# A hybrid conv / SSD diffusion layer on one core: the prompt's norm and eight projections moved ahead of the sample's norm, and the gate products of the scan moved half a chunk later

## The chip, the cores and the metric

The kernel runs on one core of one Trainium2 chip. The metric is the device time of one execution in microseconds. A kernel consists of five instruction queues that run side by side: PE (TensorE, matrix products into PSUM), DVE (VectorE), ACT (ScalarE), POOL (GpSimd, which reads and writes SBUF only) and SP (SyncE, which here only issues DMA transfers). Each queue runs its instructions in the order in which they were written into the program, and an instruction waits on semaphores for the results or free buffers it needs.

## The reference

One layer is applied to two groups of tokens with the same weights: 256 prompt tokens and 1024 sample tokens of width 1024. Cut to what matters here:

```python
mod = silu(c) @ w_ada + b_ada                         # six blocks of 1024: shift, scale, gate, twice
h   = rmsnorm(x, g_norm1) * (1 + scale_m) + shift_m   # over 1024 channels
hc, gb, gc, z, xbc, dtf, dtb = split(h @ w_in)        # 512, 512, 512, 512, 1024, 8, 8 columns
out_a = gb * dwconv1d(gc * hc)                         # short gated convolution
xs, B, C = split(silu(dwconv1d(xbc) + b))              # 512, 256, 256
dt  = softplus(dt + dt_bias); y = ssd(xs, dt, B, C)    # chunks of 128 tokens, forward and backward scan
y   = rmsnorm(y * silu(z), g_ssd_norm)
x   = x + gate_m * (concat(out_a, y) @ w_out)
x   = x + gate_f * convffn(rmsnorm(x) * (1 + scale_f) + shift_f)
```

The prompt uses the modulation of `c_ctx`, the sample that of `c`. The results are the final norms of both groups and the prompt's two final scan states.

## The kernel before, in words

Activations lie transposed: channels on the 128 partitions, tokens along the free dimension. So `x` is eight tiles ("channel blocks", k = 0 to 7) of 128 channels, and a matrix product with `w_in` gives an output tile of 128 channels as a sum over the eight k. Products are made in three passes to keep precision: a weight tile is split into a rounded high part (`whi`, on ScalarE) and the rest (`wlo`, on VectorE or GpSimd), the activation likewise, and TensorE adds high x high, high x low and low x high (`mm3`, L160, L162, L164; all three kinds of operation are recorded at the lines of small helpers such as L77, `tt`, and L80, `stt`). A prompt tile is thus 8 x 3 = 24 products of 256 columns, a sample tile 48 products of 512 columns. `w_in` has 24 output tiles: 12 for the short convolution (`outa`, three for each j), 4 for `z` (`zproj`), 8 for `xbc`; a narrow product gives dt.

The order of the work around the change is the order of the code, arranged by a list scheduler within it (each engine's queue can take a later piece of code first where its inputs are earlier), and by a few hand-set edges (`after`).

1. *Start* (L232 to L264). Both groups' `x` are loaded, ScalarE squares them, TensorE sums the squares over the channels with a matrix of ones (L243, L256), ScalarE makes the reciprocal root by Ln and Exp.
2. *The channel loop* (L310 to L339). For each k, `ada_block(k)` (L277 to L296) loads two pieces of the first two modulation blocks, multiplies them (L284), transposes the result (L290) and makes `mod` and `aff`, the scale of the norm. Then the sample's block k is normalized and split (L320 to L324), and two of the sample's `xbc` tiles (`N_LOOP = 2`) get their products for this k (L332). The prompt's block is normalized as well (L335), and the sample's dt products run at k = 3 and 7.
3. *Prompt tiles*: eight `xbc` tiles (L703), four `z` tiles with the prompt's dt stage (`dtstage`, a chain of small operations between ScalarE and VectorE), and twelve tiles of `outa`.
4. *Sample tiles*: its dt stage, the other six `xbc` tiles (L731), with the other four modulation blocks (`ada`) between them.
5. *The scan.* While chunks of the scan run, `fillers` gives TensorE halves of the sample's `z` and `outa` tiles. `gate(x, c0, n)` makes the norm of `y * silu(z)` of one chunk in three steps: load z; multiply, square and add; sum over channels on TensorE (L800), Ln, Exp and multiply. `post_s(i)` says after which half chunk i each step is written. Then come `w_out` and the feed-forward part.

The tile pools hand out buffers by tag: the PSUM pool has `acc` (two tiles of 1024 columns), `yp` (one) and `sa` (three). A new tile waits until its buffer's last reader is done.

## Time and profile before

| | |
|---|---|
| three runs | 1577.93, 1579.02, 1580.55 us (median 1579.02) |
| profiled execution | 1580.42 us, of which the span from first to last instruction is 1578.5 us |
| granted TensorE clock, mean | 0.991 |
| busy: PE, DVE, ACT, POOL | 1525.0, 1101.3, 662.0, 513.8 us |
| DMA | 191.98 MB, mean 122 GB/s |
| first product of step 3 / L458 of step 4 / first product of `w_out` | 71.2 / 157.5 / 516.1 us |

A row of the timeline has the start in us, the duration in us, the engine, the line, the operation, output and input tiles (numbers left out) with shapes, and how many records were merged; in brackets stands the idle time of the engine before it and what ended it. Two records belong to one product of 32-bit floats with full precision. TensorE's records overlap, so the distance of two starts is the price of one. A row by windows gives, for a stretch of the execution, busy time and number of instructions of PE, PEld (the weight loads), DVE, ACT and POOL, and then the granted clock (1.00 is full speed), the DMA engines' mean busy share and GB/s.

### The profile page before, as it was taken

What the parts mean: (1) busy time and instruction counts of PE and PEld (TensorE: products, weight loads), DVE (VectorE), ACT (ScalarE), POOL (GpSimd) and SP (SyncE); (2) the same over time, 40 slices, a digit from 0 to 9 for tenths busy, and PEclk for the clock granted to TensorE, in tenths of its full rate; (3) what the DMA queues carried; (4) which work ended last, traced back from release to release, by engine and by line L of the source; (5) the groups of instructions that cost most, each with busy time, mean ns of one, the idle gap of its engine ahead of it and who ended that gap; (6) DMA issues with size and microseconds to landing.
All of it is one profiled execution on the core that took longest, in us unless ns stands there. A gap on an engine that the chain in (4) does not pass through costs nothing. (4 is left out here: it accounts for less than half of the span.)

```text
span 1578.5 us, 22525 instructions
## 1 busy us (share of the span) xinstructions
PE 1525.0 (97%) x8722; PEld 1296.2 (82%) x8722; DVE 1101.3 (70%) x1634; ACT 662.0 (42%) x1025; POOL 513.8 (33%) x288
## 2 busy tenths in 40 slices
PE   6988999999999999999999999999999999999997
PEld 2688667777877888888888888888888888888886
DVE  5665615367787339797666598656679978798696
ACT  6553334257777235443332253332334433433333
POOL 1455001111110001343333333333346555445452
PEclk9999999999999999999999999999999999999999
DMA  8555554343434712322222233212252322343221
GB/s 304 214 184 162 216 202 147 111 150 123 144 101 146 286 67 82 112 73 69 66 68 78 66 133 112 70 65 67 76 184 93 102 99 99 106 161 97 93 78 61
DMA packets 86908, 191.98 MB, mean 122 GB/s; under 512 B 9330, under 2 KB 36626, under 8 KB 86802
## 3 DMA queue, kind: packets, MB, share of 16 engines
q1 hardware_dynamic: 80978, 187.41, 34.6%
q10 hardware_dynamic: 5824, 3.15, 0.7%
q8 instruction: 68, 1.11, 0.3%
q14 instruction: 38, 0.31, 0.1%
HBM read 167.37 MB, written 23.15 MB: 121 GB/s over the span
## 5 line engine op out<-in xcount | busy, mean ns | idle before, releaser
L80 DVE SCALAR_TENSOR_TENSOR cc<-acc,sm,cc 128x504 f32<-128x504 f32 (+5 forms) x836 | 545.7, 665 | 110.8 <-ACT cc L983 52.5
L77 POOL TENSOR_TENSOR wlo<-raw,whi 128x1024 fp32r<-128x1024 f32 (+2 forms) x83 | 193.5, 2331 | 672.4 <-ACT whi L151 518.5
L151 ACT ACTIVATE whi<-raw 128x1024 fp32r<-128x1024 f32 x90 | 95.1, 1057 | 243.6 <-PE acc L162 215.6
L80 DVE SCALAR_TENSOR_TENSOR x<-dn,mod,x 128x288 f32<-128x288 f32 (+2 forms) x176 | 96.1, 546 | 95.3 <-PE dn L164 95.1
L77 POOL TENSOR_TENSOR dlo<-draw,dhi 128x512 fp32r<-128x512 f32 (+1 forms) x88 | 108.9, 1238 | 90.8 <-ACT dhi L1036 88.8
L160 PE MATMUL acc<-ya,whi 128*128 128x512 f32 (+1 forms) x400 | 119.2, 355 | 1.4 <-DVE cv L77 1.4
L162 PE MATMUL acc<-ya,whi 128*128 128x512 f32 (+1 forms) x400 | 119.0, 355 | 0.0
L162 PE MATMUL acc<-oa,whi 128*128 128x512 f32 (+1 forms) x400 | 118.9, 355 | 0.0
L164 PE MATMUL acc<-ya,wlo 128*128 128x512 f32 (+1 forms) x400 | 118.7, 354 | 0.0
L164 PE MATMUL acc<-oa,wlo 128*128 128x512 f32 (+1 forms) x400 | 118.6, 354 | 0.0
L160 PE MATMUL acc<-oa,whi 128*128 128x512 f32 (+1 forms) x400 | 118.4, 353 | 0.0
L160 PE MATMUL dn<-yb,dhi 128*128 128x288 f32 (+2 forms) x352 | 110.0, 313 | 5.3 <-DVE x L80 4.1
L77 POOL TENSOR_TENSOR wlx<-raw,whx 128x1024 fp32r<-128x1024 f32 (+2 forms) x32 | 73.7, 2303 | 120.2 <-ACT whx L151 104.5
L162 PE MATMUL dn<-yb,dhi 128*128 128x288 f32 (+2 forms) x352 | 109.6, 311 | 0.8 <-POOL yb L77 0.8
L164 PE MATMUL dn<-yb,dlo 128*128 128x288 f32 (+2 forms) x352 | 109.6, 311 | 0.0
L160 PE MATMUL acc<-h,whi 128*128 128x512 f32 x320 | 105.7, 407 | 0.0
L1036 ACT ACTIVATE dhi<-draw 128x512 fp32r<-128x512 f32 (+1 forms) x88 | 52.9, 602 | 121.5 <-PE dn L162 50.8
L162 PE MATMUL acc<-h,whi 128*128 128x512 f32 x320 | 101.4, 396 | 0.0
L164 PE MATMUL acc<-h,wlo 128*128 128x512 f32 x320 | 100.8, 396 | 0.0
L160 PE MATMUL dn<-g,dhi 128*128 128x288 f32 (+2 forms) x304 | 95.1, 313 | 0.0
L162 PE MATMUL dn<-g,dhi 128*128 128x288 f32 (+2 forms) x304 | 94.8, 312 | 0.3 <-POOL g L77 0.3
L164 PE MATMUL dn<-g,dlo 128*128 128x288 f32 (+2 forms) x304 | 94.8, 312 | 0.0
(340 smaller groups left out, 3628.9 us busy)
## 6 DMA issues: line engine op xcount, KB each, us to landing
raw<-in_w_up SPq DMA_DIRECT2D x88, 512.0 KB, 3.2
x<-in_w_ada SPq DMA_DIRECT2D x32, 512.0 KB, 5.5
draw<-in_w_down SPq DMA_DIRECT2D x64, 256.0 KB, 2.7
x<-in_w_in SPq DMA_DIRECT2D x24, 512.0 KB, 3.3
raw<-in_w_in SPq DMA_DIRECT2D x22, 512.0 KB, 4.2
xs<-in_w_ad SPq DMA_DIRECT2D x16, 512.0 KB, 8.4
csb<-csds SPq DMA_DIRECT2D x16, 512.0 KB, 3.8
raw<-in_w_out SPq DMA_DIRECT2D x16, 512.0 KB, 3.2
```

What stands on the lines that cost most here:

```text
L77: (eng or V).tensor_tensor(out=out, in0=a, in1=b, op=op)
L80: V.scalar_tensor_tensor(out=out, in0=a, scalar=s, in1=b, op0=op0, op1=op1)
L151: act(hi, raw, AF.Copy)
L160: nc.tensor.matmul(o, wh[:, k, :], rh(k), start=k == 0, stop=False)
L162: nc.tensor.matmul(o, wh[:, k, :], rl(k), start=False, stop=False)
L164: mm = nc.tensor.matmul(o, wl[:, k, :], rh(k), start=False, stop=k == n - 1)
L1036: act(wh, raw, AF.Copy)
```

## The change

- *Start.* Only the prompt's `x` is loaded and normalized first. The table that holds Ln and Exp is loaded once, early.
- *Channel loop.* For each k, the modulation block, the prompt's normalized block and the products of **all eight prompt `xbc` tiles** for this k (L301; eight 256-column halves of four PSUM tiles of a new tag `pj`, five buffers). The weight piece of a block is 512 KB in place of 128 KB; its low part is made by VectorE. Behind it, the sample's block of `x` is loaded, squared on ScalarE and added up by **GpSimd**.
- *Sample's norm.* `norm_s`, a generator: sums by TensorE, Ln, Exp, then for each k one `stt` on VectorE (x times scale times factor), one activation (the high part), one `stt` (the low part). Its steps are called between the prompt's `z` and `outa` tiles. The shift is left out of the sample's `x`, so its dt product gets the shift's part by eight one-column products.
- *Prompt tiles.* `xbc` reads the PSUM tiles of the loop. All other prompt tiles use `pj`, and their weights are loaded into four pieces of `xq`.
- *Sample tiles.* All eight `xbc` tiles are here now, and the dt products before them, in a new PSUM pool.
- *The scan.* Step three of `gate` for chunk c - 1 and the prompt's gate steps are written after other half chunks; at the end, the splits of `y` and the last three fillers are written in another order. PSUM pools wait tile by tile where one takes another's place.

```diff
-N_LOOP = 2
...
-        if "space" not in kw:
+        if kw.get("space") != DRAM:
             kw["reuse_waits"] = "tile"
...
+    def pj():
+        return T(ps, [P, 512], "pj", 5)
...
-    xs = [T(nrm, [P, TS], "x", 8) for _ in range(KT)]
-    pr_s = [psa(), psa()]
-    for k in range(KT):
-        dma(xs[k], xT[:, k, TP:TT])
-        q = T(cv, [P, TS], "cv", 4)
-        sq = act(q, xs[k], AF.Square)
...
+    pl = [pj() for _ in range(4)]
+    pxbc = [pl[t // 2][:, TP * (t % 2):TP * (t % 2) + TP] for t in range(8)]
+    xs = []
+    ada_block(0)
+    for k in range(KT):
+        raw = T(wst, [P, KT, P], "raw", 2)
+        dma(raw, A["w_l"][k])
+        wh, wl = wpair()
+        act(wh, raw, AF.Copy)
+        tt(wl, raw, wh.bitcast(F32), ALU.subtract)
+        if k < KT - 1:
+            ada_block(k + 1)
+        q, i = k // 4, k % 4
+        hi, x = hp_hi[q][:, i], xp[q][:, i]
+        act(hi, x, AF.Identity, scale=aff[:, 0, k, 0:1], bias=col(0, k, 0))
+        ts(x, x, aff[:, 0, k, 0:1], col(0, k, 0), ALU.mult, ALU.add)
+        tt(hp_lo[q][:, i], x, hi.bitcast(F32), ALU.subtract)
+        for n, (w, h) in enumerate(((wh, hi), (wh, hp_lo[q][:, i]), (wl, hi))):
+            for t in range(8):
+                mm = nc.tensor.matmul(pxbc[t], w[:, t, :], h, ...)
...
+        x = T(nrm, [P, TS], "x", 8)
+        dma(x, xT[:, k, TP:TT])
+        xs.append(x)
+        sq = T(hsp, [P, TS], "h", 16)
+        act(sq, x, AF.Square)
+        if k == 0:
+            acc_s = sq
+        else:
+            tt(acc_s, acc_s, sq, ALU.add, nc.gpsimd)
...
+    def norm_s():
+
+        rs = T(cv, [P, TS], "cv", 4)
+        for a in range(0, TS, 512):
+            pr = psa()
+            nc.tensor.matmul(pr, ones, acc_s[:, a:a + 512], start=True, stop=True)
+            act(rs[:, a:a + 512], pr, AF.Ln, scale=1.0 / D, bias=epsc)
+            act(rs[:, a:a + 512], rs[:, a:a + 512], AF.Exp, scale=-0.5)
+        for k in range(KT):
+            x = xs[k]
+            stt(x, x, aff[:, 0, k, 1:2], rs, ALU.mult, ALU.mult)
+            hi, lo = [T(hsp, [P, TS], "h", 16, F32R) for _ in range(2)]
+            act(hi, x, AF.Identity, bias=col(0, k, 1))
+            stt(lo, x, col(0, k, 1), hi.bitcast(F32), ALU.add, ALU.subtract)
...
+            yield
...
     for j in range(4):
         zproj(SP, j, PG if j % 2 else PV)
         if j == 0:
             dts = dtstage(SP, d4_p, silu)
+        else:
+            next(norm)
     for j in range(4):
-        for _ in outa(SP, j, PG):
-            pass
-        if j == 0:
+        for i, _ in enumerate(outa(SP, j, PG)):
+            if i % 4 == 1:
+                next(norm, None)
+        if j == 1:
             dttok(SP, *dts)
+    for _ in norm:
+        pass
+    close_pool(g_ps)
...
-    for i in range(N_LOOP, 7):
+    for i in range(7):
         xbc(SS, i, xbcs[i], PV)
...
         if i == 0:
-            next(gate_p)
             next(gates[0])
-        if i == 1:
-            next(gate_p)
         if i % 2 == 1:
             next(gates[c])
-        else:
             if c > 0:
                 next(gates[c - 1])
             if c + 1 < SS.nc:
                 next(gates[c + 1])
+        if i in (0, 3):
+            next(gate_p)
...
-    with tc.high_priority():
-        next(gates[-1])
-    for _ in filler:
-        pass
...
+    split(xall, mya, 0)
+    split(xq[:, :, 0:TA - TP], mya, TP)
+    next(filler)
+    next(filler)
+    next(gates[-1])
+    for _ in filler:
+        pass
+    split(xq[:, :, TA - TP:], myb, 0)
```

The instruction queues show where things stand now. First ScalarE in the channel loop, before. `h` is the sample's normalized high part, `bc` the prompt's, `whi`/`whx` a weight's high part, `cv<-sa` the copy of the modulation products:

```order
L314 ACTIVATE whi_248<-raw_246 128x256
L287 ACTIVATE cv_216<-sa_207 128x256
L321 ACTIVATE h_225<-x_113,mod_80,aff_81 128x1024
L335 ACTIVATE bc_173<-xl_100,mod_80,aff_81 128x256 x2
L314 ACTIVATE whx_293<-raw_291 128x256
L287 ACTIVATE cv_263<-sa_254 128x256
L321 ACTIVATE h_272<-x_114,mod_80,aff_81 128x1024
```

The same place in the change; `h<-x` is now the square of the sample's x:

```order
L271 ACTIVATE cv_220<-sa_211 128x256
L311 ACTIVATE h_257<-x_255 128x1024
L296 ACTIVATE bc_119<-xl_101,mod_78,aff_79 128x256
L290 ACTIVATE whx_262<-raw_260 128x1024
L271 ACTIVATE cv_277<-sa_268 128x256
L311 ACTIVATE h_314<-x_312 128x1024
L296 ACTIVATE bc_119<-xl_101,mod_78,aff_79 128x256
L290 ACTIVATE whi_319<-raw_317 128x1024
```

A block's weight split (L290) stood ahead of its modulation copy and norm (L314 before); it stands behind the norm (L296) now, and a square lies between copy and norm.

Then VectorE behind the prompt's dt stage, at the first `outa` tiles, before (`acc` is PSUM; `cv`, `xl`, `sm` are SBUF):

```order
L77 TENSOR_TENSOR cv_1072<-acc_1080,cv_1072 128x256
L80 SCALAR_TENSOR_TENSOR cv_1106<-cv_1072,sm_63,cv_1106 128x255 x2
L520 TENSOR_SCALAR cv_1155<-cst_66,cep_934 40x40 x2
L77 TENSOR_TENSOR cv_1106<-acc_1116,cv_1106 128x256
L77 TENSOR_TENSOR xl_1144<-cv_1106,xl_1142 128x256
L77 TENSOR_TENSOR cv_1193<-acc_1201,cv_1193 128x256
```

And in the change (`x` the sample's block, `cv_731` the norm's factor, `h` high and low part, `pj` PSUM):

```order
L79 SCALAR_TENSOR_TENSOR x_199<-x_199,aff_79,cv_731 128x1024
L79 SCALAR_TENSOR_TENSOR x_255<-x_255,aff_79,cv_731 128x1024
L79 SCALAR_TENSOR_TENSOR x_312<-x_312,aff_79,cv_731 128x1024
L79 SCALAR_TENSOR_TENSOR h_742<-x_199,mod_78,h_741 128x1024
L79 SCALAR_TENSOR_TENSOR h_780<-x_255,mod_78,h_779 128x1024
L79 SCALAR_TENSOR_TENSOR x_369<-x_369,aff_79,cv_731 128x1024
L79 SCALAR_TENSOR_TENSOR h_818<-x_312,mod_78,h_817 128x1024
L76 TENSOR_TENSOR cv_851<-pj_863,cv_851 128x256
L79 SCALAR_TENSOR_TENSOR x_426<-x_426,aff_79,cv_731 128x1024
L79 SCALAR_TENSOR_TENSOR h_855<-x_369,mod_78,h_854 128x1024
```

The reader of the first `outa` group's second tile (`cv_851<-pj_863`) comes behind seven of the norm's sixteen operations, that of its third tile behind fourteen.

Last TensorE in the scan, before, around a gate's sum (L800; `acc` a half tile of the fillers):

```order
L606 MATMUL sa_3122<-bc_1524,bc_1522 128x128
L160 MATMUL acc_3153<-h_225,whi_3149 128x512 x2
L162 MATMUL acc_3153<-h_228,whi_3149 128x512 x2
L164 MATMUL acc_3153<-h_225,wlo_3150 128x512
L800 MATMUL sa_3139<-cv_2983,ones_70 128x128 x2
```

In the change, where it is L814 (`yp` is the scan's output):

```order
L657 MATMUL yp_3197<-wm_3137,xd_3065 64x128
L657 MATMUL yp_3197<-csb_3049,sfw_2970 64x128
L657 MATMUL yp_3197<-csb_3049,sb_3051 64x128
L814 MATMUL sa_3317<-cv_3006,ones_70 128x128 x2
L160 MATMUL acc_3253<-h_931,whi_3249 128x512 x2
L162 MATMUL acc_3253<-h_932,whi_3249 128x512 x2
```

The sum stood five products into the first half of a filler tile; it stands behind that whole half (24 rows of products, the first ones on `h_741`) and the next twelve products of the scan's output, of which the fence shows the last three.

More of the change, by code (lines that the diff above doesn't have):

```diff
@@ L230, in body @@
     xT = A["xT"]
+    tab = lnexp_table(first)
+    after(act(arow, rows[:, 0:1], AF.Exp), tab)
+    ts(arow, arow, -1.0, None, ALU.mult, ALU.bypass)
     xp = [T(cv, [P, 4, TP], "xl", 2) for _ in range(2)]
```

155 lines of the change are left out of this document (59 added, 96 removed).

## The prediction

> **What bounds the kernel now.** I read the page's busy shares first, then the table of TensorE's waits, then the timelines of the engines up to 172 us.
>
> ```profile
> PE 1525.0 (97%) x8722; PEld 1296.2 (82%) x8722; DVE 1101.3 (70%) x1634; ACT 662.0 (42%) x1025; POOL 513.8 (33%) x288
> ```
>
> Of TensorE's waits (total, count, longest) these are the ones that matter here:
>
> ```profile
> PE yp L243 <- DVE cv L77: 10.9, 1, 10.9
> PE sa L800 <- DVE cv L77: 6.4, 4, 3.2
> PE acc L160 <- DVE cv L77: 1.4, 1, 1.4
> PE sa L800 <- ACT btok L540: 0.7, 1, 0.7
> ```
>
> TensorE bounds the program; only 53.5 us of the 1578.5 us span are idle. They put 10.9 us at the start and 6.4 + 0.7 + 1.4 = 8.5 us around the gates of the scan (L800) and the step to `wout`. The change touches these two places and leaves everything from `wout` on as it is.
>
> ```profile
> 77.95 0.28 PE L162 MATMUL sa<-bc,whi 128*128 128x256 f32 x1
> 78.07 0.28 PE L164 MATMUL sa<-bc,wlo 128*128 128x256 f32 x1
> 102.71 0.62 PE L458 MATMUL sa<-cv,cst 128*40 128x256 f32 x2
> 157.48 1.91 PE L458 MATMUL sa<-raw,cst 128*40 128x512 f32 x4
> 159.32 0.74 PE L160 MATMUL acc<-h,whx 128*128 128x512 f32 x2
> 169.97 0.62 PE L164 MATMUL acc<-h,wlx 128*128 128x512 f32 x2
> 170.53 3.64 PE L177 MATMUL sa<-x,sc 128*32 128x512 f32 x32
> ```
>
> Two neighbouring prompt products start 0.12 us apart, so a prompt tile (24) is worth 2.88 us. A sample tile (48 products, two per row at 0.457) is worth 24 x 0.457 = 10.95 us. By 102.7 us the eight prompt `xbc` tiles and two sample tiles are done; the other 16 prompt tiles run to 157.5 (54.8 us for 46.1 of products), and then sample's own part begins with L458. I compare the two kernels at that point.
>
> **Loop of the change.** Per channel block: eight modulation products, 24 prompt products, a weight split, one square.
>
> ```profile
> 57.15 1.07 PE L284 MATMUL sa<-xs,sc 128*32 128x256 f32 x16
> 58.66 0.38 ACT L287 ACTIVATE cv<-sa 128x256 f32<-128x256 f32 x1 [1.19 <-PE sa L284]
> 60.25 1.24 ACT L321 ACTIVATE h<-x,mod,aff 128x1024 fp32r<-128x1024 f32 x1 [1.20 <-DVE aff L83]
> 61.40 0.59 ACT L335 ACTIVATE bc<-xl,mod,aff 128x256 fp32r<-128x256 f32 x1
> 61.89 1.04 ACT L151 ACTIVATE whx<-x 128x1024 fp32r<-128x1024 f32 x1
> ```
>
> When loads arrive is read from the squares that wait for them:
>
> ```profile
> 7.85 1.06 ACT L238 ACTIVATE cv<-xl 128x1024 f32<-128x1024 f32 x1 [0.42 <-DMA xl<-in_xT]
> 9.34 1.06 ACT L249 ACTIVATE cv<-x 128x1024 f32<-128x1024 f32 x1 [0.43 <-DMA x<-in_xT]
> 18.73 1.06 ACT L249 ACTIVATE cv<-x 128x1024 f32<-128x1024 f32 x1 [0.27 <-DMA x<-in_xT]
> ```
>
> From the end of the modulation products (58.22) to the normalized activation (60.25) are 2.03 us; the prompt's activation takes 0.5 until the next one starts, the split of a weight 1.04. In the changed order ScalarE has block k+1's weight split right behind its normalized activation, and TensorE has the modulation products of k+1 after 14 prompt products of block k. So the blocks follow each other by 14 x 0.12 + 1.07 + 0.15 (sequencing) + 2.03 + 0.5 + 1.04 = 6.5 us, against 4.4 us of products. The loads don't set this: eight pieces of x land in 9.39 us, 1.34 us per 512 KB, and a block moves four (two of modulation, x, weights: 5.4 us). The larger weight pieces (512 KB for 128) are hidden by those 1.1 us; at a rate a quarter lower each block would cost 0.2 us more. On SyncE's queue each load waits at most for products or splits two blocks back.
>
> Start: two loads of the prompt, then two of modulation, one of weights and two of modulation end near 7.9 + 5 x 1.34 = 14.6 us (7.85 is the second load of the prompt); the first two blocks share one chain to `aff`. With 1 to 2 us of modulation products, 2 to 2.6 us of chain, the first 24 products (2.9 us, 5.8 at half clock) and the third block's chain, block 2 starts between 27 and 33 us; I take 30. Then 5 x 6.5, and 3.8 us for the last block's low part and products: the loop ends at **66 us**. Adding two sample tiles (21.9) gives 88 where now 102.7 stands, and 3.6 us of sample's dt products (the L177 row's kind) come later: **-11 us** so far.
>
> **The 16 prompt tiles with sample's norm.** Here I expect the loss.
>
> ```profile
> 138.51 2.40 POOL L77 TENSOR_TENSOR wlo<-x,whi 128x1024 fp32r<-128x1024 f32 x1 [0.48 <-ACT whi L151]
> 138.86 2.85 DVE L80 SCALAR_TENSOR_TENSOR cv<-cv,sm,cv 128x255 f32<-128x255 f32 x2 [0.94 <-ACT cv L431]
> 155.78 1.01 DVE L80 SCALAR_TENSOR_TENSOR cv<-cv,sm,cv 128x255 f32<-128x255 f32 x2 [0.58 <-ACT cv L431]
> 26.00 1.23 DVE L77 TENSOR_TENSOR x<-x,cv 128x1024 f32<-128x1024 f32 x1 [1.59 <-ACT cv L262]
> 26.35 1.46 POOL L77 TENSOR_TENSOR wlo<-raw,whi 128x256 fp32r<-128x256 f32 x1 [1.34 <-ACT whi L314]
> 27.22 1.67 DVE L77 TENSOR_TENSOR x<-x,cv 128x1024 f32<-128x1024 f32 x1
> 141.81 0.42 DVE L77 TENSOR_TENSOR cv<-acc,cv 128x256 f32<-128x256 f32 x1
> 165.80 1.22 DVE L80 SCALAR_TENSOR_TENSOR cv<-cv,cv 40x1024 f32<-40x1024 f32 x1
> ```
>
> Two VectorE operations with both inputs in SBUF take 1.01 us alone and 2.85 us when GpSimd's 2.40 us subtraction runs: they end 0.80 us after it (141.71 against 140.91), so they stood still. At 26 us the turn is the other way, then alternates: 1.23, GpSimd, 1.67. With an input in PSUM (141.81) nothing is lost. So such work adds up on the two engines.
>
> The norm puts 16 scalar-tensor-tensor operations of 128x1024 there, 1.22 us each, 19.5 us. Under GpSimd's 2.4 us per tile they must alternate. ScalarE's queue holds each next weight split behind a normalized activation that waits for VectorE, and the PSUM tiles that TensorE needs are freed by operations queued behind the norm: so the last tile's split waits for nearly all of it.
>
> Counted from the loop's end. The first tiles: six evacuations and two splits on ScalarE (6 x 0.5 + 0.4 + 2 x 1.04), then GpSimd's 2.4, so full pace from 7.5; z0 to z2 8.6, two products for the norm's sum 1.8, half clock after the gap 2.5: z2 ends near 20.4. The dt chain (L472 to L493) took 8.9 us, much of it behind GpSimd:
>
> ```profile
> 108.70 0.42 ACT L472 ACTIVATE cv<-cv 40x256 f32<-40x256 f32 x1
> 117.63 0.42 ACT L493 ACTIVATE cv<-cv 40x256 f32<-40x256 f32 x1 [4.44 <-DVE cv L492]
> 24.50 0.68 ACT L261 ACTIVATE cv<-sa,epsc 128x512 f32<-128x512 f32 x1
> 25.33 0.64 ACT L262 ACTIVATE cv<-cv 128x512 f32<-128x512 f32 x1
> 18.49 5.42 PE L256 MATMUL sa<-cv,ones 128*128 128x512 f32 x12 [0.53 <-DVE cv L77]
> ```
>
> (Twelve records are six products, 0.9 us each.) It starts at 18.5, ends near 26, and the four Ln and Exp (2.6 us) stand behind it: the norm's factor is ready at 29. From there to the last split: ten GpSimd subtractions (24.0), 15 norm operations (18.3), three times `outa`'s two operations and one subtraction (4.3), and ScalarE's steps that neither engine covers (3 to 4): 29 + 50 = 79, and 2 us of the last tile: **81 us** in place of 54.8, **+26**. Sample's dt bias (eight small products, copies and a transfer to the next matmul) and a third PSUM tile that waits for the dt stage: **+2**.
>
> **The scan.** In the rows by windows the last three columns are granted clock, DMA share and GB/s.
>
> ```profile
> 380.83 1.19 PE L800 MATMUL sa<-cv,ones 128*128 128x128 f32 x4 [3.21 <-DVE cv L77]
> 384.00:386.00 2.00, 2.00 (x6) 1.61 (x5) 0.69 (x1) 2.00 (x8) 0.00 (x0) 0.50 0.04 14
> 30.55 1.30 PE L332 MATMUL acc<-h,whi 128*128 128x512 f32 x4 [2.12 <-ACT h L321]
> 36.00:38.00 2.00, 2.00 (x6) 1.59 (x5) 2.00 (x2) 1.60 (x2) 0.00 (x0) 0.50 0.79 278
> ```
>
> The gates' sum products move behind 24 products and 12 outputs of the next half (some 7 us), and the last gate gets fillers on both sides. That is more than the longest wait, so the 8.5 us go; so does the half clock that followed the 3.21 us gap, about 6 us of it, 3 us. Some of it the next limit keeps: **-9** (bounds -12 and -4).
>
> Priced at nothing: the earlier table load (ScalarE idles for the first load anyway; 1.3 us if not), the PSUM pools' finer waits, and the new pool between prompt and sample (covered by the sum above; a microsecond if not).
>
> Sum: -11 + 26 + 2 - 9 = **+8 us**. The profiled execution took 1580.42 us with a span of 1578.5, the median is 1579.02: 1587 us.
>
> The clock: after the 2.12 us gap above the granted clock was 0.50 at 36 to 38 us. The loop has 2.1 us idle per 6.5 us block, in two pieces, so half clock may hold there. The Trainium skill (TensorE: Matmul & The Clock Gate, Part 1) has the clock halve only after an idle window of some 3.4 us; by it the loop keeps full clock and the sum stays +8. The trace disagrees in so far as 2.12 us were enough; I leave that case a chance.
>
> **Rivals.**
> 1. *Sample's norm hides.* If GpSimd gets ahead while VectorE waits for something else, TensorE sets the pace: 7.5 + 46.1 + 1.8 + 2.5 + 0.6 = 58.5 us for the 16 tiles, 22 less: **1565 us**. For it: GpSimd has only 14 x 2.4 = 34 us of work in the 81. Against it: from 29 us on the shared work is without a gap. It decides once the factor is ready ten microseconds earlier, or VectorE isn't held. Faster than before below 73 us.
> 2. *GpSimd's sums of squares block `aff`.* The square ends within 0.1 us of the moment when `mod` and `aff` are due on VectorE; if the 2.4 us sum goes first, each of five blocks takes 8.9: +12, **1599 us**. For it: the alternation at 26 us. Against it: the copy stands ahead of the square on ScalarE.
> 3. *Half clock through the loop*: 14 x 0.12 + 1.07 + 0.5 doubled is +3.3 per block, +16: **1603 us**.
>
> **Numbers.** Forecast 0.50, its own range 1577 to 1597; rival 1 0.27, rival 2 0.15, rival 3 0.08. A measurement here tells about 0.2% (3.2 us) from no change. Faster: nearly all of rival 1 and a little of the forecast, 0.31; within 0.2%: 0.12; slower: 0.57. The range reaches to rival 1 and rival 3: 1565 to 1603.
>
> **What would show it.** Right: loop blocks 6 to 7 us apart, its last product near 66; sixteen tiles in 75 to 85 us with VectorE and GpSimd together busy almost all of it and TensorE waiting for POOL `wlo` or DVE; no L814 wait above 0.5 us. Wrong: sample's L457 products before 140 us, which leaves the norm hidden.

## The result, and the profile after

The change made the kernel slower: 1595.29 us (median of 6 runs, 1591.33 to 1598.77) against 1579.76 us (1577.93 to 1583.04) of the kernel before on the same chip, a ratio of 1.0096 (95% interval 1.0081 to 1.0111). The profiled execution took 1594.92 us with a span of 1592.8 us; the span before was 1578.5 us, so the two traces differ by 14.3 us. The medians differ by 15.5 us. The forecast was +8 us, with a range of 1565 to 1603.

Rows of TensorE's timeline of the changed kernel (start, duration, engine, line, operation, and in brackets the idle time ahead and who ended it): three blocks of the loop, the loop's end, sample's dt products, the beginning of the scan's prompt part, and `wout`.

```profile
42.03 0.86 PE L301 MATMUL pj<-bc,whi 128*128 128x256 f32 x5 [1.60 <-ACT whi L290]
48.54 0.86 PE L301 MATMUL pj<-bc,whx 128*128 128x256 f32 x5 [1.60 <-ACT whx L290]
55.05 0.85 PE L301 MATMUL pj<-bc,whi 128*128 128x256 f32 x5 [1.60 <-ACT whi L290]
...
66.18 1.22 PE L301 MATMUL pj<-bc,wlo 128*128 128x256 f32 x8 [2.09 <-DVE wlo L76]
...
150.65 3.85 PE L324 MATMUL sa<-x,toks 128*32 128x512 f32 x26
...
258.03 0.60 PE L535 MATMUL sa<-cst,xp 128*128 128x128 f32 x4
...
527.94 0.51 PE L160 MATMUL acc<-ya,whi 128*128 128x256 f32 x2
...
540.68 0.61 PE L160 MATMUL acc<-oa,whi 128*128 128x256 f32 x2 [2.87 <-DMA oa<-oad]
```

The two rows of the kernel before that answer to the last but two and the last but one:

```profile
236.88 0.60 PE L535 MATMUL sa<-cst,xp 128*128 128x128 f32 x4
...
516.12 0.59 PE L160 MATMUL acc<-ya,whi 128*128 128x256 f32 x2 [1.41 <-DVE cv L77]
```

The loop takes 6.5 us per block and ends at 67.4 us; the 16 prompt tiles end at 150.65, 83.3 us later, in place of the 54.8 us before. At the beginning of the scan the changed kernel is 258.03 - 236.88 = 21.2 us behind. At the first product of `wout` it is 527.94 - 516.12 = 11.8 us behind, so the scan gave back 9.4 us; the longest wait at a gate's sum (L814) is 0.4 us now. Then comes a wait of 2.87 us that was not there before. At the end of the span 14.3 us are left.

TensorE's largest waits of the changed kernel between 60 and 150 us (total, count, longest), and two rows by windows from there (length, then busy time and instructions of TensorE, its weight loads, VectorE, ScalarE and GpSimd, then granted clock, DMA share and GB/s):

```profile
PE sa L523 <- DVE cv L520: 5.9, 1, 5.9
PE pj L164 <- POOL wlo L76: 5.1, 2, 2.7
PE pj L160 <- ACT cv L422: 4.4, 1, 4.4
PE pj L160 <- ACT whx L151: 4.1, 2, 2.4
```

```profile
100.00:120.00 20.00, 17.00 (x118) 16.55 (x119) 20.00 (x10) 8.99 (x9) 15.25 (x6) 0.85 0.37 127
120.00:140.00 20.00, 9.72 (x53) 9.17 (x52) 19.80 (x20) 9.18 (x15) 9.35 (x4) 0.75 0.15 50
```

VectorE is busy all the time here, and TensorE about two thirds of it, at three quarters to 0.85 of its clock.

### The profile page after: what moved, and what is told of

It reads as the page before. It is cut to its first block, busy times and chain, and to the rows that moved or that the text cites. A ratio compares the mean times of both kernels' runs of the same rounds, so it can differ in the third digit from the quotient of the medians.

```text
span 1592.8 us, 22475 instructions
## 1 busy us (share of the span) xinstructions
PE 1520.4 (95%) x8724; PEld 1299.9 (82%) x8724; DVE 1119.8 (70%) x1635; ACT 658.2 (41%) x1017; POOL 509.4 (32%) x280
## 5 line engine op out<-in xcount | busy, mean ns | idle before, releaser
L76 POOL TENSOR_TENSOR wlo<-raw,whi 128x1024 fp32r<-128x1024 f32 (+1 forms) x77 | 186.9, 2427 | 658.7 <-ACT whi L151 539.5
L160 PE MATMUL acc<-h,whi 128*128 128x512 f32 x352 | 114.1, 403 | 0.0
L162 PE MATMUL acc<-h,whi 128*128 128x512 f32 x352 | 110.9, 395 | 0.0
L164 PE MATMUL acc<-h,wlo 128*128 128x512 f32 x352 | 110.0, 393 | 0.0
L76 POOL TENSOR_TENSOR wlx<-raw,whx 128x1024 fp32r<-128x1024 f32 (+1 forms) x30 | 72.0, 2400 | 113.1 <-ACT whx L151 104.5
```

Of the source, the lines that this page charges most:

```text
L76: (eng or V).tensor_tensor(out=out, in0=a, in1=b, op=op)
L160: nc.tensor.matmul(o, wh[:, k, :], rh(k), start=k == 0, stop=False)
L162: nc.tensor.matmul(o, wh[:, k, :], rl(k), start=False, stop=False)
L164: mm = nc.tensor.matmul(o, wl[:, k, :], rh(k), start=False, stop=k == n - 1)
```

## The experiments

Times are medians; a ratio is against runs of the kernel before that were measured alongside, with its 95% interval. To compare the parts, two marks are read from each profile: the first low product of the loop's last block ("loop mark", 66.18 us in the changed kernel) and sample's first dt product (150.65); the 84.5 us between them are called the tile stage. A third is the first norm operation on VectorE, when the norm's factor is ready:

```profile
96.91 7.93 DVE L79 SCALAR_TENSOR_TENSOR x<-x,aff,cv 128x1024 f32<-128x1024 f32 x3 [1.52 <-ACT cv L337]
```

### Does GpSimd hold VectorE up in the tile stage? (e2, e3, e4)

e2 puts all low parts of the prompt's weights on VectorE:

```diff
-        zproj(SP, j, PG if j % 2 else PV)
+        zproj(SP, j, PV)
...
-        for i, _ in enumerate(outa(SP, j, PG)):
+        for i, _ in enumerate(outa(SP, j, PV)):
```

> The changed kernel, with the low parts of the 16 prompt tiles' weights (z and outa) all on VectorE, none on GpSimd. Theory (VectorE's operations with two SBUF inputs and GpSimd's exclude each other, so their times add up): 14 subtractions of 2.40 us go from the shared time and 14 of 1.13 come: -18 us; the stage of the 16 tiles shrinks from 83 to 65-68 us, 1577 to 1580. Rival (VectorE is simply full, 20.0 of 20 us busy, by its own operations): it gets 16 us more to do, the stage grows to 95 or more, 1605 to 1611. Second rival (ScalarE's order, or the factor that is ready only 29 us after the loop, sets the stage): no change, 1595.

e3 keeps GpSimd's work, and keeps the factor in PSUM:

```diff
-        return T(ps, [P, 512], "pj", 5)
+        return T(ps, [P, 512], "pj", 3)
+    def prs():
+        return T(ps, [P, 1024], "rs", 1)
...
-        rs = T(cv, [P, TS], "cv", 4)
+        rs = prs()
```

> The changed kernel with the norm's factor kept in PSUM (a tile of 1024; the ring of pj tiles shrinks from 5 to 3): the first of each block's two norm operations reads one input from PSUM, the second stays as it is. GpSimd keeps its subtractions. Theory (exclusion only where both inputs are in SBUF): 8 operations of 1.22 us run beside GpSimd, the stage is 8 to 10 us shorter, less up to 3 us for the shorter ring: 1586 to 1590. Rival (VectorE is full by its own operations): the same number of operations of the same size, no change, or slower by the shorter ring: 1595 to 1598.

The norm's two operations in the groups by line and shape (x8 each; busy time, mean ns of one), of the changed kernel, of e2 and of e3:

```profile
L79 DVE SCALAR_TENSOR_TENSOR h<-x,mod,h 128x1024 fp32r<-128x1024 f32 x8 | 18.7, 2345 | 0.2 <-ACT h L342 0.2
L79 DVE SCALAR_TENSOR_TENSOR x<-x,aff,cv 128x1024 f32<-128x1024 f32 x8 | 18.6, 2345 | 1.5 <-ACT cv L337 1.5
```

```profile
L79 DVE SCALAR_TENSOR_TENSOR h<-x,mod,h 128x1024 fp32r<-128x1024 f32 x8 | 10.1, 1279 | 0.0
L79 DVE SCALAR_TENSOR_TENSOR x<-x,aff,cv 128x1024 f32<-128x1024 f32 x8 | 10.1, 1279 | 0.2 <-ACT cv L337 0.2
```

```profile
L79 DVE SCALAR_TENSOR_TENSOR h<-x,mod,h 128x1024 fp32r<-128x1024 f32 x8 | 13.0, 1635 | 0.0
L79 DVE SCALAR_TENSOR_TENSOR x<-x,aff,rs 128x1024 f32<-128x1024 f32 x8 | 10.0, 1265 | 0.0
```

That settles that the lock exists (a VectorE operation with both inputs in SBUF stands still while GpSimd works on SBUF) and what it costs an operation. The same operations take 2345 ns beside GpSimd and 1279 ns without it. In e3 GpSimd works as before, and the operation whose factor now lies in PSUM falls to 1265 ns, while its neighbour with both inputs in SBUF stays longer (1635, down from 2345). Of the 37.3 us of the two groups, 17.1 were standing still.

The times: e2 1585.24 us, ratio 1.0027 (1.0012 to 1.0042); e3 1581.34 us, 1.0012 (0.9998 to 1.0026), against 1.0096 of the change. From the ready factor to sample's dt products there are 53.7 us in the changed kernel, 44.3 in e2 and 41.1 in e3. e2 gained less than the 18 us that the theory gave: without GpSimd VectorE itself is full (9.80 of 10 us busy between 94 and 104, 10.00 in the next ten), so the rival was right about that and wrong about its price. e3 gained 13 us by the ratios, where its expectation had 5 to 9. The stage is 72.1 us in e2 and 69.7 in e3, against 84.5: the lock is worth 12 to 15 us of it, and without it the stage is still some 14 us longer than the 54.8 us of the kernel before (the loop mark lies 1.2 us ahead of the loop's end).

e4 leaves the 16 operations out (ScalarE makes one tile per block, so the sample's activations lack the norm; products, loads and splits stay):

```diff
-            stt(x, x, aff[:, 0, k, 1:2], rs, ALU.mult, ALU.mult)
-            hi, lo = [T(hsp, [P, TS], "h", 16, F32R) for _ in range(2)]
-            act(hi, x, AF.Identity, bias=col(0, k, 1))
-            stt(lo, x, col(0, k, 1), hi.bitcast(F32), ALU.add, ALU.subtract)
+            hi = lo = T(hsp, [P, TS], "h", 16, F32R)
+            act(hi, x, AF.Identity, scale=rs[:, k:k + 1], bias=col(0, k, 1))
```

> The changed kernel without the 16 norm operations on VectorE between the prompt tiles: ScalarE still makes one normalized tile per block, sample's high and low parts are both that tile, so sample's activations lack the norm and the low part (the output is not the reference's). All products, loads and splits stay. Theory (the norm on VectorE alone makes the loss of the stage): the 16 tiles take 58 to 62 us in place of 83, 1570 to 1574. Rival (the stage is also late by the loop's end, ScalarE's order or cold TensorE): it shrinks by less than 15 us, 1581 or more.

1585.20 us, 1.0033 (1.0021 to 1.0044). The stage shrank from 84.5 to 76.5 us only, as the rival said: with VectorE idle 9.6 of 10 us between 94 and 104, TensorE still stands. Rows of ScalarE and TensorE in e4, and its row by windows:

```profile
94.13 3.49 ACT L341 ACTIVATE h<-x,mod,cv 128x1024 fp32r<-128x1024 f32 x3
...
98.92 1.04 ACT L151 ACTIVATE whx<-xs 128x1024 fp32r<-128x1024 f32 x1
...
100.01 0.58 PE L160 MATMUL pj<-bc,whx 128*128 128x256 f32 x1 [6.49 <-ACT whx L151]
```

```profile
94.00:104.00 10.00, 2.36 (x9) 2.06 (x10) 0.42 (x1) 10.00 (x11) 3.96 (x2) 0.62 0.11 25
```

In e4 the weight split `whx` stands behind four normalized activations on ScalarE, and these wait for the factor. That order is e4's own. In the changed kernel the split that comes when the factor is ready stands ahead of the first normalized activation:

```profile
96.78 1.04 ACT L151 ACTIVATE whx<-xs 128x1024 fp32r<-128x1024 f32 x1
98.23 1.15 ACT L342 ACTIVATE h<-x,mod 128x1024 fp32r<-128x1024 f32 x1 [0.41 <-DVE x L79]
```

So e4 shows that ScalarE's queue behind a late factor can hold the stage too, and that the stage isn't short by itself when VectorE is free. It doesn't show how long the changed kernel's stage would be without the norm's operations: e3, which keeps them all, has the shorter stage.

### Is it the late factor? (e7)

The factor is made right behind the loop, in the code ahead of everything else of the prompt:

```diff
+    rs = T(cv, [P, TS], "cv", 4)
+    for a in range(0, TS, 512):
+        pr = psa()
+        nc.tensor.matmul(pr, ones, acc_s[:, a:a + 512], start=True, stop=True)
+        act(rs[:, a:a + 512], pr, AF.Ln, scale=1.0 / D, bias=epsc)
+        act(rs[:, a:a + 512], rs[:, a:a + 512], AF.Exp, scale=-0.5)
     def norm_s():
-        rs = T(cv, [P, TS], "cv", 4)
-        for a in range(0, TS, 512):
...
```

> The changed kernel, with sample's norm factor (two products, Ln, Exp) computed right behind the loop, ahead of the prompt's evacuations' SiLU, instead of behind z0 to z2 and the dt chain; nothing left out. Theory (the stage is the sum of VectorE's and GpSimd's shared work, of which 50 us wait until the factor is ready 29 us after the loop): the norm starts near 70 us, so the idle shared time before 97 us is used; the stage shrinks from 83 to 70-74 us, 1582 to 1586. Rival (the place of the norm operations in VectorE's and ScalarE's queues, not the factor, sets it): they then only block the first tiles' splits instead of the last ones', less than 4 us, 1591 or more.

1596.44 us, 1.0102 (1.0074 to 1.0130): no gain. The first norm operation starts at 75.28 us in place of 96.91, and yet the stage is 83.5 us. VectorE is now full from 75 to 105 us (10.00, 9.89 and 10.00 of 10), and the dt chain, whose small operations stand between the norm's, is late for the decay product of `dttok`, at which TensorE waits 5.9 us, as long as in the changed kernel. The rival is right for this order: with an early factor the norm's operations hold up the first tiles (GpSimd's second subtraction starts at 90.11 us, against 81.60 in the changed kernel).

### What sets the loop's period? (e5, e12, e13, e15)

Each block of the changed kernel waits 1.6 us for its weight split, which stands behind the normalized activation on ScalarE. e5 makes the split one block earlier:

```diff
+    ada_block(0)
+    nxt = lweights(0)
     for k in range(KT):
+        wh, wl = nxt
+        if k == 0:
+            ada_block(1)
+            nxt = lweights(1)
+        elif k < KT - 1:
+            nxt = lweights(k + 1)
             ada_block(k + 1)
```

Here `lweights` holds the raw load of a block's weights, their split and their low part, and the copy in `ada_block` is ordered behind that split.

> The changed kernel, with the next block's weights split ahead of the next modulation's copy on ScalarE in the loop (the wh tile is made one block earlier in the code and the copy is ordered behind it); nothing left out. Theory (each block waits 1.6 us for its weight split because ScalarE does it behind the normalized activation): the period falls from 6.5 to 5.0-5.4 us (there the loads of 2 MB a block, 5.1 us at 410 GB/s, become the limit), the loop ends 5 to 8 us earlier, 1587 to 1590. Rival (the loads set the period already, or the chain from the modulation products to the activation gets as much longer): no change, 1595.

1604.20 us, 1.0146 (1.0112 to 1.0179): 8 us slower than the change. The wait for `whi` was gone, but the edit also moved the modulation's loads behind the weights', and with them the modulation products behind 14 and 23 of a block's 24 products. One block of e5 and its window:

```profile
48.11 1.21 PE L314 MATMUL pj<-bc,whi 128*128 128x256 f32 x8 [1.36 <-ACT bc L309]
50.38 1.65 PE L314 MATMUL pj<-bc,whi 128*128 128x256 f32 x6 [1.07 <-DVE bc L76]
```

```profile
45.00:55.00 10.00, 7.43 (x42) 5.00 (x34) 3.90 (x6) 2.88 (x4) 2.37 (x1) 0.67 0.59 194
```

The granted clock fell to 0.67 and the period rose to 10.5 us. A reduced clock in the loop was the third rival of the prediction; it came here, in e5. How much of the 4 us more per block is the clock, and how much the later modulation products, was not separated. e12 keeps the modulation's loads ahead of the weights':

```diff
+            wa = ada_load(k + 1)
+            nxt = lweights(k + 1)
+            ada_block(k + 1, wa, nxt[2] if k > 0 else None)
```

> The changed kernel with the weight split ahead of the modulation's copy on ScalarE as in e5, but with the modulation's loads issued ahead of the weights' again, so that TensorE has the modulation products of the next block in the first ten products of a block, not behind 22; nothing left out. Theory (e5 lost because the modulation products moved behind most of the block's products and the clock fell to 0.67; without that the weight split's 1.6 us go): period 5.0 to 5.6 us at full clock, loop end 5 to 7 us earlier, 1588 to 1590. Rival (several short waits per block, even if shorter in sum, halve the clock): period 7 or more, 1598 to 1605.

1587.75 us, 1.0044 (1.0031 to 1.0057), the time that was expected, but not for the reason. The period is 6.9 us, not 5.0 to 5.6. VectorE and GpSimd in one block of e12:

```profile
49.14 1.57 DVE L76 TENSOR_TENSOR mod<-mod,sm 128x4 f32<-128x4 f32 x1
```

```profile
48.34 2.35 POOL L76 TENSOR_TENSOR h<-h,h 128x1024 f32<-128x1024 f32 x1 [4.54 <-ACT h L323]
```

The addition for `mod`, 0.16 us alone, ends at 50.71, just after GpSimd's sum of squares at 50.69: the second rival of the prediction. In the changed kernel that addition starts at 46.48, 0.35 us ahead of the sum, which waits for a square that ends at 46.69; in e12 it starts 0.80 us behind the sum. e13 puts the sums on VectorE, behind the prompt's low part:

```diff
-            tt(acc_s, acc_s, sq, ALU.add, nc.gpsimd)
...
+        if k > 1:
+            add = V.tensor_tensor(out=acc_s, in0=acc_s, in1=sq, op=ALU.add)
+            after(add, low)
```

> e12 with the loop's seven sums of squares on VectorE (behind the prompt's low part) instead of GpSimd; nothing left out. Theory (in e12 each block loses 1.4 us where VectorE's addition for mod waits for GpSimd's sum, and the transposes' place costs the rest): period 6.9 to 5.5 us, loop end 8 us earlier than e12's 68, 1578 to 1581. Rival (the period is set by the loads or by TensorE's order): no change, 1588.

1578.58 us, 0.9988 (0.9974 to 1.0002). The period is 5.47 us, and the loop mark comes at 60.10 us against e12's 67.44:

```profile
41.68 1.46 PE L316 MATMUL pj<-bc,whi 128*128 128x256 f32 x10 [0.79 <-ACT bc L308]
47.15 1.44 PE L316 MATMUL pj<-bc,whx 128*128 128x256 f32 x10 [0.79 <-ACT bc L308]
```

So the period had two limits one behind the other, weight split and GpSimd's sum, and taking one away gives nothing without the other. e15 makes the second edit alone, in the loop of the changed kernel:

> The changed kernel with only the loop's sums of squares on VectorE instead of GpSimd; nothing left out. Theory (in the changed kernel as it is, the additions for mod and aff come just ahead of GpSimd's sum, and only the prompt's scaling, 1.76 in place of 0.42 us, waits for it, off the path to the weight split): period stays 6.5 us, no change in the loop, 1594 to 1596. Rival (the sums on GpSimd delay the loop, the second rival of the prediction): period 5 to 6, 1587.

1584.87 us, 1.0023 (1.0012 to 1.0033), 10 us better than expected. The period stays at 6.5 us, as the theory said. Most of the gain comes behind the loop. Rows of ScalarE and TensorE of the changed kernel, and then of e15:

```profile
69.70 1.09 ACT L151 ACTIVATE whx<-xs 128x1024 fp32r<-128x1024 f32 x1
...
70.84 0.39 PE L160 MATMUL pj<-bc,whx 128*128 128x256 f32 x1 [2.44 <-ACT whx L151]
...
75.33 0.58 PE L164 MATMUL pj<-bc,wlo 128*128 128x256 f32 x1 [2.75 <-POOL wlo L76]
```

```profile
60.57 1.04 ACT L151 ACTIVATE whx<-xs 128x1024 fp32r<-128x1024 f32 x1
...
64.56 0.39 PE L160 MATMUL pj<-bc,whx 128*128 128x256 f32 x1
```

Without the 2.09 us in which the last block's low part waited behind GpSimd's last sum, and with another order of ScalarE's instructions (the first prompt tile's split is ahead of the six evacuations of the loop, not behind them), the first tile follows at once. The product that opens the prompt's dt stage follows the first tile at 67.59 in e15, and the first two tiles, which run interleaved, at 80.43 in the changed kernel, 5.2 and 14.3 us behind the loop mark. e5, e12, e13 and e15 all have the first split ahead of the evacuations, and tile stages of 75.1 to 76.4 us against 84.5, without an edit of the tiles.

What this start is worth was not measured alone, since the order of VectorE and ScalarE further on moved with it. In these four runs the factor is ready 27.6 to 28.2 us behind the loop mark, against 30.7, so some 3 of the 8 to 9 us are gained ahead of the factor. The others are gained behind it: 47.4 to 48.3 us to the sample's dt products, against 53.7, with nine of GpSimd's subtractions left in place of ten. One subtraction less (2.4 us) can be a part of that; the rest stays open.

### The scan, and the new wait at wout (e1, e6, e11)

e1 is the kernel before with the change's `post_s` and its order of splits and last fillers:

```diff
-        if i == 1:
-            next(gate_p)
...
+        if i in (0, 3):
+            next(gate_p)
...
+    split(xall, mya, 0)
+    split(xq[:, :, 0:TA - TP], mya, TP)
+    next(filler)
+    next(filler)
+    next(gates[-1])
+    for _ in filler:
+        pass
+    split(xq[:, :, TA - TP:], myb, 0)
```

> The kernel before with only the scan's part of the change: the gates' order in post_s, the fillers and splits behind the scan. Prompt, sample and the loop stand as before. Theory (the waits of the gates' sum products, 8.5 us with the half clock behind them, go, and nothing else of the change matters for it): the first wout product comes 9 us earlier than before, of which some 3 us are lost again where the products of wout wait for the last oa loads, since the changed order puts the last yb splits ahead of the last filler's own work on VectorE and ScalarE: -6 us, about 1573.5. Rival (the scan's gain came from the PSUM pools' finer waits or from where sample's part stands): 0, about 1580.

1577.01 us, 0.9977 (0.9965 to 0.9988). The part of the change that was worth 9.4 us in the changed kernel is worth 3.6 us here by the ratio, and 6.0 us at the first product of `wout` (9 had been expected there):

```profile
510.09 0.59 PE L160 MATMUL acc<-ya,whi 128*128 128x256 f32 x2 [3.38 <-DVE cv L77]
```

The waits at the gates are gone, but the first product waits 3.38 us for a PSUM tile, since the kernel before lets a new PSUM pool wait for the old one as a whole. In the changed kernel the pools wait tile by tile, that wait is gone, and the loads of `oa` are late instead. e6 is the changed kernel with the last `yb` splits ordered behind the last filler's high and low part:

```diff
-    split(xq[:, :, TA - TP:], myb, 0)
+    split(xq[:, :, TA - TP:], myb, 0, True)
...
+            if late:
+                after(h, last_hi[0])
+                after(l, last_lo[0])
```

> The changed kernel, with the last chunk's yb splits ordered behind the last filler's high and low part on ScalarE and VectorE; nothing left out. Theory (the 2.9 us wait for the last oa loads at wout comes from these splits, 2.6 and 2.7 us, ahead of the last filler's work): the wait at the first product with oa is gone, -2.9 us, 1592. Rival (the loads themselves, or the store to memory and back, set it): the wait stays, 1595.

The wait fell from 2.87 to 1.23 us:

```profile
535.63 0.62 PE L160 MATMUL acc<-oa,whi 128*128 128x256 f32 x2 [1.23 <-DMA oa<-oad]
```

In the changed kernel, the four `yb` splits stood ahead of the filler's last operations on VectorE:

```profile
527.47 2.74 DVE L79 SCALAR_TENSOR_TENSOR yb<-xs,sm,yb 128x512 fp32r<-128x512 f32 x4 [0.79 <-ACT yb L860]
530.13 1.22 DVE L76 TENSOR_TENSOR cv<-acc,cv 128x1024 f32<-128x1024 f32 x1
...
533.53 1.22 DVE L76 TENSOR_TENSOR xl<-cv,xl 128x1024 fp32r<-128x1024 f32 x1
```

So the cause is right for more than half of the wait; two splits of `wout`'s weights remain ahead of the low part on VectorE, and whether they make the rest was not tried. The time, 1597.45 us and 1.0094 (1.0065 to 1.0123), cannot tell 1.6 us from nothing.

e11 puts the useful pieces into the kernel before: e1's order, the finer PSUM waits, e6's order, and the prompt's `dttok` behind the last `outa` tile:

```diff
-        if j == 0:
+        if j == 3:
             dttok(SP, *dts)
```

> The kernel before with the change's scan part (e1), the PSUM pools' finer waits, the last yb splits behind the last filler (e6), and the prompt's dttok behind the last outa tile; nothing left out. Theory: e1's 1577, less the 3.4 us that the first wout product waits for the PSUM tile (finer waits), less the 4.0 us wait of the decay product in the prompt stage of the kernel before and the half clock behind it (about 3): 1567 to 1571. Rival (these waits only move, as the wait for the oa loads showed): 1574 to 1577.

1569.77 us, 0.9935 (0.9911 to 0.9958): the lowest median of this study, 10 us below the kernel before. Sample's dt stage starts at 151.3 us against 157.5 (the wait of 4.0 us for the decay product is gone, and the clock from 130 to 140 us is 1.00 in place of 0.80); 2.3 us of that are lost again in a new wait inside the dt stage, for ScalarE's `tokp`. The first product of `wout` comes at 504.63 against 516.12; 1.10 us of the wait for `oa` remain. The new order of the prompt isn't needed for any of it.

### Do the repairs add up? (e8, e9, e10, e14, e16, e17)

e8 had e5's loop, e7's early factor (copied to PSUM), e6's order and the decay product one tile later:

> The changed kernel with all of these together: weights split ahead in the loop, the factor early (then copied to PSUM by ScalarE, pj ring of 3), yb splits late, and the prompt's 40-column decay product one outa tile behind its diagonals (a wait of 5.9 us after the change). Nothing left out. If the causes are the ones named, their gains add up: loop -5 to -7, tiles -18 to -22 (to 62-65 us, where TensorE sets the pace), wout -3: 1563 to 1570, below the kernel before. If the stage has another bound that none of them touches (ScalarE's order, half clock after gaps): 1575 to 1582.

1601.46 us, 1.0131 (1.0106 to 1.0156). It inherited e5's loop (loop mark at 82.67 us); the tile stage was 73.6 us. e9 and e10 changed the tile stage alone, e9 from e3, e10 from e2 and e7, both with `dttok` behind the last tile:

> The kernel of e3 (norm factor in PSUM), with the prompt's token-major dt copies and decay product (dttok) behind the last outa tile instead of behind the second; nothing left out. Theory (what is left of the stage above 58 us is, beside the start, the wait of its decay product for VectorE's small diagonals, which stand behind the norm operations, 1.6 us in e3 and 5.9 after the change, and the half clock behind it): -2 to -4 us against e3's 1581, 1577 to 1579. Rival (the stage is the sum of VectorE's work and GpSimd's, so the wait only moves to the next product): 1581.

> Three edits together, nothing left out: all low parts of the prompt tiles on VectorE (e2), the factor early (e7), dttok behind the last outa tile. In e2 VectorE was full from 94 to 124 us and had room before; in e7 the room was used, but dttok then waited 5.9 us and half clock followed. Theory (VectorE's own work, some 60 us in all, spread over the whole stage, then lies under TensorE's 58): the stage falls from e2's 71 to 60-64 us, 1575 to 1579. Rival (the order of the queues, first tiles' splits behind norm operations, sets it): 1583 to 1590 as e2 and e7.

```diff
-        if j == 1:
+        if j == 3:
             dttok(SP, *dts)
```

e9 took 1581.77 us, 1.0008 (0.9991 to 1.0024), e10 1583.95 us, 1.0013 (0.9998 to 1.0029): nothing gained against e3 and e2. In e10 a wait of 7.7 us for ScalarE's copy of `outa`'s first product (L423) came in place of the others. Perhaps `dttok`'s tiles, held longer in the ring of four `cv` buffers that `outa` uses too, are the reason; whether they are was not tried.

e14 joins e13's loop, the transposes of the next modulation ordered ahead of a block's last eight products, e3 and e6; e16 also has the z tiles' low parts on VectorE; e17 also the early factor and the prompt's decay product one `outa` tile behind its diagonals. Of their edits, beside those shown:

```diff
+                if 0 < k < KT - 1 and n == 2 and t == 0:
+                    after(mm, turned[0])
...
-        zproj(SP, j, PG if j % 2 else PV)
+        zproj(SP, j, PV)
...
+    after(act(xall, xall, AF.Silu), rsx)
+    rs = prs()
+    for a in range(0, TS, 512):
+        act(rs[:, a:a + 512], ln[:, a:a + 512], AF.Copy)
```

The first piece is e14's, where `turned` is the last transpose of the next block's modulation; the second comes with e16; the third with e17, where `rsx` is the factor's last Exp, made in SBUF (`ln`) at once behind the loop and copied to PSUM.

> e13, with the transposes of the next modulation ordered ahead of a block's last eight products, the norm factor in PSUM (e3) and the last yb splits late (e6); nothing left out. If the named costs add up: loop at 5.1 to 5.3 us a block (then the loads set it), end near 58 us, the stage of the 16 tiles 66 to 69 us as in e3, wout -1.5: 1563 to 1568, better than e11's 1570. If the loop's gain is lost in the tile stage (whose first weights are loaded behind the loop's): 1574 or more.

> e14 with the low parts of all four z tiles on VectorE (which has room before the factor is ready), the outa tiles' on GpSimd as before; nothing left out. Theory: TensorE's waits for GpSimd's first low parts (some 3 us and the half clock behind them) go: 2 to 4 us below e14. Rival (VectorE's evacuations of xbc then wait behind these subtractions): the same as e14 or 2 us above.

> e16 with the factor made right behind the loop and copied to PSUM by ScalarE once the prompt's evacuations have freed the bank, and the prompt's decay product one outa tile behind its diagonals; nothing left out. Theory (VectorE's norm operations can start only when the factor is ready, 30 us after the loop, and then fill VectorE; earlier, they use the room before): the norm starts some 12 us earlier, TensorE's waits of 10.4 and 5.7 us shrink to less than 5 together, 1562 to 1567. Rival (the first half of the stage then waits as the second did): 1570 to 1575.

e14: 1576.90 us, 0.9978 (0.9965 to 0.9990); e16: 1572.55 us, 0.9949 (0.9933 to 0.9966); e17: 1570.74 us, 0.9945 (0.9924 to 0.9966). The loop reached 5.23 us a block with a loop mark of 55.6 to 59.1 us, as expected. The tile stage did not reach the 66 to 69 us hoped for: 80.4, 74.4 and 72.9 us. In e14 the factor is ready only 34.1 us behind the loop mark, against 28.6 in e3, and the second half of its sum waits 4.4 us for ScalarE; its two longest waits in the stage are 8.6 and 5.7 us, where e3's longest is 4.3. TensorE's largest waits in the stage of e16, and then of e17:

```profile
PE pj L163 <- DVE cv L76: 10.4, 1, 10.4
PE sa L545 <- DVE cv L542: 5.7, 1, 5.7
```

```profile
PE pj L167 <- POOL wlo L76: 4.6, 3, 2.1
PE pj L163 <- ACT whi L154: 2.5, 1, 2.5
PE pj L163 <- ACT cv L519: 2.0, 1, 2.0
```

e17's two long waits are gone, and the stage is 1.5 us shorter; VectorE is nearly full in both from 85 to 115 us (9.2 to 10.0 of 10). The new order of the prompt can thus be made 0.5% faster than the kernel before, but no kernel here with it was faster than the old order with the scan's part (e11); the intervals of e11, e16 and e17 overlap. Why the stage of e14 to e17 stays longer than e3's 69.7 us was not found.

## Why the prediction was right and wrong

**Right** were the sign and, in the main, the mechanism of each large term. The loop's period was forecast as 6.5 us and is 6.5; its end as 66 us and is 67.4. The tile stage was forecast as 81 us, by adding up the times of VectorE and GpSimd from a ready factor 29 us behind the loop; it took 83.3, with the factor at 29.5. Of GpSimd's subtractions, the forecast left ten behind the factor, and ten there are. e2 and e3 show the lock by which the times add, and that it makes 12 to 15 us of the stage. They do not show that the sum would hold in another order: without the lock the stage falls to about 70 us, not to the 58.5 of rival 1. The scan was to give back 9 us and gave 9.4. Rival 2 (GpSimd's sums) and rival 3 (half clock in the loop) did not come: the `mod` addition is 0.35 us ahead of GpSimd's sum, and the granted clock is 1.00 from 35 to 65 us.

**Wrong** was the size of the sum: +8 us forecast, 14.3 us between the traces and 15.5 between the medians. Two steps failed.

1. "The change ... leaves everything from `wout` on as it is": this put at nothing what measured 2.9 us. The change reorders the splits of `y` and the last fillers, and I priced that order by the gates alone. Their operations stand ahead of the last filler's on VectorE and ScalarE, and the store, and the load that follows it, come late at `wout`. e6 shows it for 1.6 of the 2.9 us; the cause of the rest stays open.
2. The terms up to the scan, -11 + 26 + 2 = +17 us, measured 21.2. The differences are small, but all to one side.
   - The loop's last block took 5.8 us in place of 3.8: its low part waited 2.09 us, since VectorE's subtraction took 3.39 us next to GpSimd's last sum. That leaves 1.1 us at the loop's end, as the block began 0.9 earlier than 30 + 5 x 6.5; rounding 66.3 to 66 makes it 1.4.
   - The tiles took 2.3 us more. Little of that lies at their start: products run without a stop from 75.33 us, 7.9 us behind the loop's end (the forecast said 7.5; its terms add up to 7.9), first at 0.21 us each with a granted clock of 0.61 (70 to 78 us), for which the forecast had 2.5 us. The third z tile's evacuation starts 20.3 us behind the loop's end (20.4 forecast for the tile's end), the factor is ready at 29.5 (29). The other 1.7 us lie behind the factor, 53.7 us in place of 52. The sum has no term for TensorE's wait of 5.9 us at `dttok`'s decay product; that this wait makes the difference was not shown.
   - From there to the scan, with the sample's dt step, half a microsecond remains.

**Rival 1**, that the norm hides, had a chance of 0.27 and a wrong point "from which it decides": a factor ready ten microseconds earlier. e7 had it 22 us earlier, and gained nothing. Its price, 58.5 us for the stage, was also too low for what was found here: no run came near it. It left out `dttok`'s wait, which stands in the 54.8 us before too (4.0 us), and the places of the norm's operations in the queues of ScalarE and VectorE.

What stays open: what would bring the stage from about 70 to 58 us. No kernel here went below 69.7 us from the loop mark.

## What to carry to other kernels

Work that "fits under" other tiles has to fit on each engine's queue in its order, not only in its idle time: add the busy times of engines that exclude each other, and look for what stands behind the moved operation in the same queue. Where two limits are one behind the other, an experiment that takes one away can show nothing or even a loss; take both away before a theory is dropped. Price a changed order at each place where a transfer starts behind it, also behind the end of the edited part, and a small edit of the code can move instructions elsewhere (e4, e5, e15), so compare the order of every engine before you explain a time.

## What the runs showed of the hardware

The granted clock did not follow TensorE's idle share. Two windows of e12's loop, and two rows of TensorE's timeline there:

```profile
35.00:45.00 10.00, 5.51 (x52) 3.84 (x52) 6.34 (x10) 3.76 (x6) 4.28 (x2) 1.00 0.91 326
55.00:65.00 10.00, 5.44 (x49) 4.01 (x47) 6.02 (x9) 3.19 (x6) 4.69 (x2) 1.00 0.62 206
```

```profile
51.66 1.44 PE L313 MATMUL pj<-bc,whx 128*128 128x256 f32 x10 [2.21 <-ACT bc L308]
...
58.54 1.46 PE L313 MATMUL pj<-bc,whi 128*128 128x256 f32 x10 [2.21 <-ACT bc L308]
```

In e12 TensorE is idle for 4.5 of 10 us, in one wait of 2.21 us per block and a few short ones, at full clock. In e5 it is idle for 2.6 of 10 us, in waits of 1.36 and 1.07 us that follow each other within 3.7 us, at a clock of 0.67 (its rows stand with that experiment). In the kernel before, a wait of 2.12 us was followed by 0.50 (the rows stand in the prediction), so the length of the longest wait alone does not decide either. Which property of the pattern decides was not tried. The Trainium skill (TensorE: Matmul & The Clock Gate, Part 1) has the clock halve after an idle window of some 3.4 us; no stretch without products in e5's block is that long, so the trace disagrees for e5 if the window must be idle throughout. The Trainium skill (same page, A second HAM failure mode: psum-queue depth-cycling) tells of a clock that swings with frequent short waits between groups of products; e5 fits that, but e12's block, with its 2.21 us, does not.

The lock between VectorE and GpSimd depends on where an operand lies, by operand and not by operation: beside GpSimd's subtractions it took 1265 ns with one input in PSUM (e3), and with both in SBUF 1635 (e3) and 2345 ns (the changed kernel). The Trainium skill (SBUF — State Buffer, SBUF: two separate sides) states such a lock, held for the whole instruction, for VectorE operations with two SBUF inputs; the trace agrees.
